# Moving eight bias-table matmuls to the start of a hybrid decoder block, and staging the second chunk's input in two rings

## The chip, the cores and the metric

The kernel runs on one core of one Trainium2 chip. The metric is the device time of one execution in microseconds, as the median of several runs. The profile is one further execution, taken by the hardware profiler; its span runs from the first to the last instruction. The engines are called as the profile calls them: PE (TensorE, matmuls; PEld are its weight loads), DVE (VectorE), ACT (ScalarE), POOL (GpSimd) and SP (SyncE, which here only issues DMAs). ACT issues some DMAs too, on a queue of its own.

## What is computed

One layer of a decoder block on 2048 positions of width 1024, in float32. The input is normalised and projected once; three mixers (a state-space mixer, a convolution module and a sliding-window attention) read parts of that projection; their outputs go through one output projection and a gate.

```python
hn = rms_norm(x, pre_norm_w)
u = jnp.einsum('bld,de->ble', hn, w_in)
z, xbc, dt_raw, conf_in, conf_gate, q, k, v, attn_gate = split_columns(u)
y_ssd = ssd_mixer(z, xbc, dt_raw, ...)
y_conf = conformer_conv(conf_in, ...) * jax.nn.silu(conf_gate)
y_attn = sliding_window_attention(q, k, v, sinks, rel_bias) * jax.nn.silu(attn_gate)
h = x + rms_norm(concat(y_ssd, y_conf, y_attn) @ w_out, post_norm_w)
return h + (p @ w_ple) * jax.nn.sigmoid(h @ w_gate)
```

The change touches the attention's relative bias: each of the eight heads adds to its scores a bias that depends only on the distance between query and key, through 32 buckets:

```python
dist = q_idx + ATTN_BLOCK - s_idx
bias = rel_bias.astype(jnp.float32)[t5_bucket(dist)]
s = jnp.where(valid, s + bias, -jnp.inf)
```

## The kernel before

**Tiling.** The 2048 positions are four chunks of 512 (`TC`). Activations lie transposed, features on the 128 partitions, so that a projection of 128 output features for one chunk is a sum over eight blocks of 128 input features (`KD`). To reach float32 accuracy with matmuls in the faster fp32r type, each operand is split into a high part and a remainder (`ah`, `al` for activations, `whi`, `wlo` for weights); `proj` issues three matmuls for each block (L443, L444, L445): low by high, high by low, high by high. For `dt` two suffice (L469, L470).

**Order.** The input projection runs in two halves of two chunks each. In a half, `head_front` projects k, v, dt, B0 and C0 for the first chunk, then for the second, and then a fixed list of units (C0, A0, S0, S1, C1, ...) each loads its weights and runs over both chunks; C is the convolution, A attention, S the state-space heads. Work that follows a projection waits in `pending` as generators, which `advance` steps once for each few matmuls. The code gives a program order; a scheduler then writes each engine's instruction list from it, by program order among what it expects to be ready. Each engine runs its list strictly in order.

**The start.** The first chunk's input is loaded in four pairs of blocks (`x_pair`, into the ring `t4`: tag "t4", four buffers of 128x1024). To begin early, `add_weighed` (ACT L392, DVE L393) multiplies it by the norm's weight only; the norm's per-position factor follows later: `sumsq_x` squares and adds (ACT L400, DVE L402), `rstd_cols` sums over partitions by matmul (L159), `make_row` transposes, stores the row to DRAM and `load_row` reads it back on all partitions (L186); it is applied when the projections leave PSUM (`evict`, DVE L478). For the second chunk, `pre_stats(1)` computes the row from another copy of the input (`xn`, also in `t4`; ACT L411), and `pre_apply(1)` loads the row into `acc`, the input pairs into the ring `gl` (two buffers), multiplies (DVE L433), and splits into `ah` and `al` (ACT L190, DVE L191).

**The bias tables.** `bias_tables` makes, for each head, one 128x384 table: a matmul of the head's 32 bucket values (and a row of -1e30 for distances out of the window), copied over 128 columns (`rbb`, DVE L547), with a one-hot matrix `oh` of 33x384. It is a float32 matmul with 33 rows, which TensorE runs in two passes (L549). ACT copies it from PSUM (L551) and SP stores it to `bias_d` in DRAM (L552), from where `attn_bias` reads it in a skewed pattern. The generator is put on `pending` after the first half's `head_front`, and uses PSUM tiles of the tag "m".

**PSUM and rings.** PSUM's eight banks are five of the tag "pp" (projections), two "m" and one "y". Other rings named below: "t" (`t512`, ten buffers of 128x512), `gl` (two) and `acc` (one).

Of the kernel before, what the change touches and what calls it, by code (L numbers as in the profile page):

```python
# [8 lines left out]
F32 = mybir.dt.float32  # L9
# [5 lines left out]
P = 128  # L15
# [3 lines left out]
TC = 512  # L19
# [3 lines left out]
NEG = -1e30  # L23
# [38 lines left out]
def hybrid_block_kernel(  # L62
# [15 lines left out]
    nc = tc.nc  # L78
    V, A, G, PE = nc.vector, nc.scalar, nc.gpsimd, nc.tensor
# [8 lines left out]
    def ps(tag):  # L88
        return psum.tile([P, TC], F32, tag=tag, name=f"ps_{tag}", bufs=PSB[tag])
# [4 lines left out]
    def t512(name, dtype=F32):  # L94
        return wk.tile([P, TC], dtype, tag="t", name=name, bufs=10)

    def t1024(name):
        return wk.tile([P, 2 * TC], F32, tag="t4", name=name, bufs=4)

    def pair(t):  # L100
        return t.rearrange("p (k t) -> p k t", k=2)

    def act_tiles():

        return act.tile([P, 2, TC], F32R, tag="ah", name="ah"), act.tile([P, 2, TC], F32R, tag="al", name="al")
# [5 lines left out]
    bias_d = dram.tile([8, P, 384], F32, name="bias_d")  # L111
# [10 lines left out]
    def pc(name, i=0, n=1):  # L122
        o, w = _par[name]
        return par_sb[:, o + i:o + i + n]
# [57 lines left out]
    def load_row(row, rb_=None):  # L182

        if rb_ is None:
            rb_ = t512("rb_")
        nc.sync.dma_start(out=rb_, in_=row.partition_broadcast(P))  # L186
        return rb_

    def split(hi, lo, src):
        A.copy(hi, src)  # L190
        V.tensor_tensor(out=lo, in0=src, in1=hi.bitcast(F32), op=ALU.subtract)  # L191
# [21 lines left out]
    pending = []  # L213
# [132 lines left out]
    with ExitStack() as c1:  # L346
        per = c1.enter_context(tc.tile_pool(name="per", bufs=1))
# [13 lines left out]
        def flush(n):  # L361
            while n > 0 and conv_q:
                if next(conv_q[0], "end") == "end":
                    conv_q.pop(0)
                else:
                    n -= 1
# [7 lines left out]
        def x_pair(c, i, tile_=None):  # L374
            x_ = pair(t1024("x2") if tile_ is None else tile_[:, 0:2 * TC])
            nc.sync.dma_start(out=x_, in_=xT[2 * i:2 * i + 2, :, c * TC:(c + 1) * TC].rearrange("k p t -> p k t"))
            return x_

        def gl_tile():
            return tp.tile([P, 30 + 2 * TC], F32, tag="gl", name="gl", bufs=2)  # L380

        def acc_tile():
            return tp.tile([P, 2 * TC], F32, tag="acc", name="acc", bufs=1)
# [35 lines left out]
        def add_pair(c, src):  # L419
            hi, lo = act_tiles()  # L420
            split(hi, lo, src)
            for kk in range(2):
                hn[c].append((hi[:, kk, :], lo[:, kk, :]))

        def pre_apply(c):

            flush(1000)
            rb_ = load_row(rows[c], acc_tile()[:, 0:TC])
            hn[c] = []
            for i in range(4):  # L430
                x_ = x_pair(c, i, gl_tile())
                for kk in range(2):
                    V.scalar_tensor_tensor(out=x_[:, kk, :], in0=x_[:, kk, :], scalar=pc("prew", 2 * i + kk), in1=rb_, op0=ALU.mult, op1=ALU.mult)  # L433
                add_pair(c, x_)


        def proj(ws, c):
# [12 lines left out]
        def wtile(name):  # L450
            return load_w(w_in[TIDX[name]])

        def dt_tile():

            st = wp.tile([P, KD, P], F32, tag="wst", name="wst", bufs=2)
            nc.sync.dma_start(out=st, in_=w_in[TIDX["dt"]])
            hi = wp.tile([P, KD, P], F32R, tag="whi", name="whi", bufs=5)
            both = wp.tile([P, KD, P], F32R, tag="wlo", name="wlo", bufs=5)
            A.copy(hi, st)
            A.copy(both, st)  # L460
            V.tensor_tensor(out=both[:, :, 16:32], in0=st[:, :, 0:16], in1=hi[:, :, 0:16].bitcast(F32), op=ALU.subtract)
            return hi, both
# [45 lines left out]
        def group_tiles():  # L508
            return tuple(per.tile([P, 2 * TC], F32, tag=n, name=n, bufs=1) for n in ("Bn", "CT", "CBm"))
# [10 lines left out]
        def bc_back(p, bT, cT, Bn, CT, CBm):  # L520
# [13 lines left out]
                in1=tri.unsqueeze(1).to_broadcast([P, NB, P]),  # L534
                op=ALU.mult,
            )


        def bias_tables():
            oh = t512("oh")  # L540
            nc.sync.dma_start(out=oh[0:33, 0:384], in_=onehot)
            rb = per.tile([33, 8], F32, name="rb")
            V.memset(rb, NEG)
            nc.sync.dma_start(out=rb[0:32, :], in_=relb)
            for h in range(8):
                rbb = t512("rbb")[0:33, 0:P]
                V.tensor_copy(rbb, rb[:, h:h + 1].to_broadcast([33, P]))  # L547
                pb = ps("m")
                PE.matmul(pb[:, 0:384], lhsT=rbb, rhs=oh[0:33, 0:384], start=True, stop=True)  # L549
                gr = t512("gr")  # L550
                A.copy(gr[:, 0:384], pb[:, 0:384])  # L551
                nc.sync.dma_start(out=bias_d[h], in_=gr[:, 0:384])  # L552
                if h % 2:
                    yield


        def dt_back(half, p, dT, dtr, tabs):
# [389 lines left out]
        for half in range(2):  # L947
            chunks = [2 * half, 2 * half + 1]
            gB = {}
            if half == 0:  # L950
                w0 = {"k": wtile("k")}
                xs = [x_pair(0, 0)]
                w0["v"] = wtile("v")
                xs += [x_pair(0, i) for i in range(1, 4)]
                w0["dt"] = dt_tile()
                w0["B0"] = wtile("B0")
                hn[0] = []
                for i in range(4):
                    add_weighed(0, xs[i], i)
                ssum = sumsq_x(xs)  # L960
                rs_ = []
            else:
                w0 = {n: dt_tile() if n == "dt" else wtile(n) for n in ("k", "v", "dt", "B0")}
                rs_ = None
            dtr = tp.tile([P, 2 * NB, 16], F32, tag="dtr", name="dtr", bufs=1)
            tabs = tuple(tp.tile([P, 2 * NB, 16], F32, tag=n, name=n, bufs=1) for n in ("dt", "acs", "eat", "dec"))
            gB[0] = group_tiles()
            front = head_front(half, 0, chunks[0], w0, gB[0], dtr, tabs, rs_)
            if half == 0:
                next(front)  # L970
                (rows[0],) = make_row(rstd_cols(ssum, 1.0 / D, EPS))
                rs_.append(load_row(rows[0]))
                for _ in pre_stats(1):
                    pass
                pre_apply(1)
            else:
                next(front)
                pre_apply(chunks[1])
            drive(front, 2)
            if half == 0:  # L980
                pre_apply(0)
            drive(head_front(half, 1, chunks[1], w0, gB[0], dtr, tabs), 2)
            if half == 0:
                pending.append(bias_tables())

            for unit in ("C0", "A0", "S0", "S1", "C1", "A1", "S2", "S3", "G1", "C2", "A2", "S4", "S5", "C3", "A3", "S6", "S7"):
                kind, j = unit[0], int(unit[1])
                if kind == "A":
                    wts = (attn_bias(j), wtile(f"q{j}"), wtile(f"ag{j}"))
                    front = attn_front  # L990
                elif kind == "C":
                    gl = gl_tile()
                    wts = (wtile(f"a{j}"), wtile(f"b{j}"), wtile(f"cg{j}"), gl)
                    front = conf_front
                elif kind == "S":
                    wts = (wtile(f"x{j}"), wtile(f"z{j}"), gB[j // 4], tabs)
                    front = ssd_front
                else:
                    gB[1] = group_tiles()
                    wts = (wtile("B1"), wtile("C1"), gB[1])  # L1000
                    front = bc_front
                for p, c in enumerate(chunks):
                    drive(front(j, p, c, *wts), TAPS[kind])
                    if half == 0 and unit == "S7" and p == 0:
                        pre_apply(2)
                    if half == 1 and unit == "S7" and p == 0:
                        tail = prep(0, YS[0])
                        pending.append(tail)
                    if half == 1 and unit == "C2" and p == 0:
                        pending.append(stats(0))  # L1010
                if half == 0 and unit == "A3":
                    keep_tail(1)
                if half == 0 and unit in ("A2", "C3"):
                    pending.append(pre_stats(j))
# [10 lines left out]
    with ExitStack() as c2:  # L1025
# [4 lines left out]
        for c in range(NCHUNK):  # L1030
# [7 lines left out]
            for n, (dp, kg) in enumerate(steps):  # L1038
# [4 lines left out]
                for kk in range(4):  # L1043
                    yh, yl = ys[4 * kg + kk]
                    first, last = kg + kk == 0, kg == 3 and kk == 3
                    for dd in range(2):
                        i = 2 * kk + dd
# [157 lines left out]
```

## Time and profile before

| | |
|---|---|
| median of 3 runs | 1844.33 us (1840.27 to 1845.91) |
| profiled execution | 1850.51 us |
| its span | 1848.7 us |
| mean granted TensorE clock | 0.994 |
| busy: PE, DVE, ACT | 98%, 75%, 44% of the span |
| L549, the tables' passes | 16, first at 100.3 us |
| L543 to L552, loads of `rb` and `oh` issued | 23.7 and 97.8 us |

A row of grouped instructions reads: line, engine, operation, output from inputs, shapes, count, then busy time, mean nanoseconds of one, and the idle time before it with what ended it. A row of the timeline reads: start and length in us, engine, line, operation; "x2" merges two in a row. A row of the chain that ended last reads: start, length, what. The letter q behind an engine means its instruction queue, which issues DMAs and waits on semaphores.

### The profile page before, as it was taken

Reading aid. Unit: us, or ns where it says so; the run is one execution under the profiler, and the core shown is the slowest. Engines: PE = TensorE matmul, PEld = TensorE weight load, DVE = VectorE, ACT = ScalarE, POOL = GpSimd, SP = SyncE. Lnnn points to the kernel's source line nnn. Section 1 sums busy time; section 2 is a strip of 40 time slices with the busy share of each in tenths; the row PEclk is TensorE's granted clock in tenths of the full one; section 3 lists DMA queues with packets and bytes.
Section 4 is the critical chain, followed back from the end, with each engine's and each line's share of the span. In section 5 each row is a group of like instructions: output and inputs, shape, how many; then the busy total and the mean of one; then the engine's idle time right before and its main releaser. Section 6 shows DMA issues by size and latency. Waiting matters only on the chain.

```text
span 1848.7 us, 25168 instructions
## 1 busy us (share of the span) xinstructions
PE 1810.7 (98%) x9386; PEld 1461.6 (79%) x9386; DVE 1385.1 (75%) x2400; ACT 818.6 (44%) x1565; POOL 0.2 (0%) x4
## 2 busy tenths in 40 slices
PE   6999999999999999999999999999999999999998
PEld 5877787787888778878788887877888788887887
DVE  6859769759869875976975996988777867466543
ACT  5525425524726542542653371465444444343331
POOL 0000000000000000000000000000000000000000
PEclk9999999999999999999999999999999999999999
DMA  7443233224433433333332332346677766578554
GB/s 234 132 133 98 80 102 96 61 78 106 171 112 111 121 102 104 91 87 89 100 115 76 101 99 87 82 145 230 214 242 236 245 228 199 202 240 280 189 188 131
DMA packets 118982, 265.09 MB, mean 143 GB/s; under 512 B 12619, under 2 KB 20428, under 8 KB 118860
## 3 DMA queue, kind: packets, MB, share of 16 engines
q1 hardware_dynamic: 108428, 246.65, 40.9%
q10 hardware_dynamic: 10432, 16.83, 4.1%
q8 instruction: 74, 1.21, 0.3%
q14 instruction: 48, 0.39, 0.1%
HBM read 205.05 MB, written 39.50 MB: 132 GB/s over the span
## 4 chain that ended last, share of the span: by engine, by line
PE 78%; DMA 8%; DVE 6%; ACT 4%; issue 2%; ACTq 1%; SPq 0%; DVEq 0%
PE ps_pp L443 15%; PE ps_pp L444 14%; PE ps_pp L445 14%; PE ps_pp L1048 4%; PE ps_pp L1049 4%; PE ps_pp L1050 4%; PE ps_pp L208 3%; PE ps_pp L209 3%; PE ps_pp L207 3%; PE ps_m L766 2%; PE ps_y L940 2%; PE ps_y L838 2%; DMA Ab<-acs_d 2%; PE ps_y L937 2%; PE ps_m L816 1%
## 5 line engine op out<-in xcount | busy, mean ns | idle before, releaser
L443 PE MATMUL ps_pp<-al,whi 128*128 128x512 f32 x1344 | 536.6, 400 | 13.6 <-DVE al L393 10.4
L444 PE MATMUL ps_pp<-ah,wlo 128*128 128x512 f32 x1344 | 534.5, 398 | 0.0
L445 PE MATMUL ps_pp<-ah,whi 128*128 128x512 f32 x1344 | 534.1, 397 | 0.0
L191 DVE TENSOR_TENSOR wlo<-wst,whi 128x1024 fp32r<-128x1024 f32 x214 | 234.1, 1102 | 179.8 <-ACT whi L190 179.4
L443 PEld LDWEIGHTS ps_pp<-al,whi 128*128 128x128 f32 x1344 | 254.4, 189 | 73.1 <-DVE al L393 10.4
L190 ACT CAST whi<-wst 128x1024 fp32r<-128x1024 f32 x214 | 202.9, 951 | 242.0 <-DMA wst<-in_w_gate_dram 86.1
L691 DVE SCALAR_TENSOR_TENSOR acc<-gl,par_sb,acc 128x1024 f32<-128x1024 f32 x240 | 307.3, 1280 | 2.3
L444 PEld LDWEIGHTS ps_pp<-ah,wlo 128*128 128x128 f32 x1344 | 254.6, 189 | 55.8 <-issue 6.5
L445 PEld LDWEIGHTS ps_pp<-ah,whi 128*128 128x128 f32 x1344 | 254.5, 189 | 54.4 <-issue 4.9
L489 DVE SCALAR_TENSOR_TENSOR cv<-raw,par_sb,cv 128x512 f32<-128x512 f32 x144 | 107.6, 747 | 22.7 <-ACT cv L487 22.0
L208 PE MATMUL ps_pp<-ah,wlo 128*128 128x512 f32 x256 | 100.2, 391 | 3.7 <-DVE wlo L191 3.7
L1048 PE MATMUL ps_pp<-bl,whi 128*128 128x512 f32 x256 | 101.5, 399 | 0.6 <-ACT whi L190 0.6
L1048 PE MATMUL ps_pp<-al,whi 128*128 128x512 f32 x256 | 100.4, 393 | 0.7 <-DVE al L191 0.7
L1049 PE MATMUL ps_pp<-bh,wlo 128*128 128x512 f32 x256 | 101.1, 395 | 0.0
L1050 PE MATMUL ps_pp<-bh,whi 128*128 128x512 f32 x256 | 100.7, 394 | 0.0
L207 PE MATMUL ps_pp<-al,whi 128*128 128x512 f32 x256 | 100.1, 391 | 0.6 <-ACT whi L190 0.5
L1049 PE MATMUL ps_pp<-ah,wlo 128*128 128x512 f32 x256 | 100.1, 391 | 0.0
L1050 PE MATMUL ps_pp<-ah,whi 128*128 128x512 f32 x256 | 100.0, 390 | 0.0
L209 PE MATMUL ps_pp<-ah,whi 128*128 128x512 f32 x256 | 99.7, 389 | 0.0
L796 ACT ACTIVATE S<-S,nm 128x256 f32<-128x256 f32 (+1 forms) x128 | 62.8, 492 | 80.0 <-DVE nm L782 74.6
L903 ACT ACTIVATE Ab<-Ab,acs 128x128 f32<-128x128 f32 x256 | 82.4, 391 | 0.4
L937 PE MATMUL ps_y<-Ab,xd 128*64 128x128 f32 x512 | 61.5, 282 | 2.0 <-issue 2.0
(235 smaller groups left out, 2592.1 us busy)
## 6 DMA issues: line engine op xcount, KB each, us to landing
wst<-in_w_in_dram SPq DMA_DIRECT2D x88, 512.0 KB, 3.5
wst<-in_w_out_dram SPq DMA_DIRECT2D x64, 512.0 KB, 5.1
Ab<-acs_d SPq DMA_DIRECT2D x64, 256.0 KB, 4.5
ysd<-y_d SPq DMA_DIRECT2D x32, 512.0 KB, 5.5
wst<-in_w_gate_dram SPq DMA_DIRECT2D x32, 512.0 KB, 3.5
gl<-in_xT_dram SPq DMA_DIRECT2D x16, 512.0 KB, 4.0
qh<-qh ACTq DMA_DIRECT2D x64, 128.0 KB, 2.4
ql<-ql ACTq DMA_DIRECT2D x64, 128.0 KB, 2.4
```

The costliest lines, as they stand in the source:

```text
L190: A.copy(hi, src)
L191: V.tensor_tensor(out=lo, in0=src, in1=hi.bitcast(F32), op=ALU.subtract)
L207: PE.matmul(out, lhsT=hi[:, k, :], rhs=al, start=start and k == 0, stop=False)
L208: PE.matmul(out, lhsT=lo[:, k, :], rhs=ah, start=False, stop=False)
L209: PE.matmul(out, lhsT=hi[:, k, :], rhs=ah, start=False, stop=stop and k == nk - 1)
L443: PE.matmul(o_, lhsT=hi[:, k, :], rhs=al, start=k == 0, stop=False)
L444: PE.matmul(o_, lhsT=lo[:, k, :], rhs=ah, start=False, stop=False)
L445: PE.matmul(o_, lhsT=hi[:, k, :], rhs=ah, start=False, stop=k == KD - 1)
L691: V.scalar_tensor_tensor(out=acc, in0=gl[:, k:k + 2 * TC], scalar=pc("ccw", j * 31 + k), in1=acc, op0=ALU.mult, op1=ALU.add)
L1048: PE.matmul(pj[dd], lhsT=hi[:, i, :], rhs=yl, start=first, stop=False)
L1049: PE.matmul(pj[dd], lhsT=lo[:, i, :], rhs=yh, start=False, stop=False)
L1050: PE.matmul(pj[dd], lhsT=hi[:, i, :], rhs=yh, start=False, stop=last)
```

## The change

The tables are computed at the start. `bias_tables` now runs up to its `yield` before `proj` is even defined, ahead of the first projection in program order: its two small loads go to ACT's DMA queue; `rbb` for all eight heads is one copy into a `gl` buffer; the eight matmuls write to eight different PSUM tiles, five "pp", two "m" and the one "y"; odd ones are evicted by DVE, even ones by ACT; four results lie in `t` buffers, two in `acc` and two in the other `gl` buffer. The stores to `bias_d` are placed after `pre_stats(1)`.

Since the `gl` ring is used by that, `pre_apply(1)` gets its four input pairs ready-made: the first two in `gl`, the other two in `t4`, all four issued ahead of the row load. The other calls of `pre_apply` stay as they were.

```diff
-        def pre_apply(c):
+        def pre_apply(c, xs=None):
 
             flush(1000)
             rb_ = load_row(rows[c], acc_tile()[:, 0:TC])
             hn[c] = []
             for i in range(4):
-                x_ = x_pair(c, i, gl_tile())
+                x_ = xs[i] if xs else x_pair(c, i, gl_tile())
...
+        def bias_tables():
+
+            rb = per.tile([33, 8], F32, name="rb")
+            nc.scalar.dma_start(out=rb[0:32, :], in_=relb)
+            oh = t512("oh")
+            nc.scalar.dma_start(out=oh[0:33, 0:384], in_=onehot)
+            V.memset(rb[32:33, :], NEG)
+            rbb = gl_tile()[0:33, 0:2 * TC].rearrange("p (h d) -> p h d", d=P)
+            V.tensor_copy(rbb, rb.unsqueeze(2).to_broadcast([33, 8, P]))
+            pairs = [acc_tile(), gl_tile()]
+            grs = [t512("gr")[:, 0:384] if h < 4 else pairs[h // 2 - 2][:, h % 2 * 384:(h % 2 + 1) * 384] for h in range(8)]
+            for h, gr in enumerate(grs):
+                pb = ps("pp" if h < 5 else "m" if h < 7 else "y")
+                PE.matmul(pb[:, 0:384], lhsT=rbb[:, h, :], rhs=oh[0:33, 0:384], start=True, stop=True)
+                if h % 2:
+                    V.tensor_copy(gr, pb[:, 0:384])
+                else:
+                    A.copy(gr, pb[:, 0:384])
+            yield
+            for h, gr in enumerate(grs):
+                nc.sync.dma_start(out=bias_d[h], in_=gr)
+
+        tables = bias_tables()
+        next(tables)
...
-        def bias_tables():
-            oh = t512("oh")
-            nc.sync.dma_start(out=oh[0:33, 0:384], in_=onehot)
-            rb = per.tile([33, 8], F32, name="rb")
-            V.memset(rb, NEG)
-            nc.sync.dma_start(out=rb[0:32, :], in_=relb)
-            for h in range(8):
-                rbb = t512("rbb")[0:33, 0:P]
-                V.tensor_copy(rbb, rb[:, h:h + 1].to_broadcast([33, P]))
-                pb = ps("m")
-                PE.matmul(pb[:, 0:384], lhsT=rbb, rhs=oh[0:33, 0:384], start=True, stop=True)
-                gr = t512("gr")
-                A.copy(gr[:, 0:384], pb[:, 0:384])
-                nc.sync.dma_start(out=bias_d[h], in_=gr[:, 0:384])
-                if h % 2:
-                    yield
...
-                pre_apply(1)
+                next(tables, None)
+                pre_apply(1, [x_pair(1, i, gl_tile() if i < 2 else None) for i in range(4)])
...
-            if half == 0:
-                pending.append(bias_tables())
```

## The prediction

> **What bounds the kernel now.** I read the page first (shares, then the chain that ended last), then TensorE's waits, the chain and the timeline of the first 120 us, and busy times by stretch.
>
> ```profile
> span 1848.7 us, 25168 instructions
> PE 1810.7 (98%) x9386; PEld 1461.6 (79%) x9386; DVE 1385.1 (75%) x2400; ACT 818.6 (44%) x1565; POOL 0.2 (0%) x4
> PE 78%; DMA 8%; DVE 6%; ACT 4%; issue 2%; ACTq 1%; SPq 0%; DVEq 0%
> ```
>
> TensorE is busy 98% of the span and carries 78% of the chain: a microsecond taken from its stream is a microsecond of the time, unless it comes out of one of its waits. Within the first 150 us the list of waits by engine and line (total, times, longest) shows two over 0.4 us:
>
> ```profile
> PE ps_pp L443 <- DVE al L393: 10.4, 1, 10.4
> PE ps_pp L443 <- DVE al L191: 3.2, 1, 3.2
> ```
>
> The first is the load of the first inputs and weights; into it the change moves work. The second is the wait for the second chunk's activations. How TensorE runs around both, and at the bias tables (columns: stretch, then busy us and count for PE, PEld, DVE, ACT, POOL, then granted clock, DMA share, GB/s):
>
> ```profile
> 10.44:17.05 6.61, 6.57 (x15) 4.53 (x16) 5.96 (x9) 6.61 (x12) 0.00 (x0) 1.00 0.94 344
> 17.05:24.70 7.65, 7.65 (x35) 6.35 (x34) 5.85 (x9) 7.22 (x12) 0.00 (x0) 1.00 0.73 244
> 41.60:45.07 3.47, 0.28 (x3) 0.00 (x1) 3.47 (x6) 2.21 (x3) 0.00 (x0) 0.90 0.26 60
> 45.07:51.10 6.03, 6.03 (x16) 4.86 (x17) 5.17 (x9) 1.07 (x2) 0.00 (x0) 0.50 0.54 173
> 112.60:116.10 3.50, 3.50 (x9) 2.83 (x9) 0.69 (x1) 1.47 (x3) 0.00 (x0) 0.51 0.67 221
> ```
>
> Full-speed 512-column matmuls come every 0.23 us (chain rows below). From 10.44 to 17.05 only 14 start (the count of 15 takes in the one at the border): half speed and two stalls, though the clock column, which knows nothing before the first recorded change, says 1.00. After the second wait 6.0 us run at a granted 0.50, and from 112.6 on 3.5 us at 0.51.
>
> **The change part by part.**
>
> *The tables leave their old place.* The chain there (start, us, what):
>
> ```profile
> 100.40 0.84 PE ps_m L549 x2
> 101.24 0.43 PE ps_pp L443
> 101.67 0.24 PE ps_pp L444
> ...
> 111.84 0.84 PE ps_m L549 x2
> 112.68 0.72 PE ps_pp L443
> 113.41 0.43 PE ps_pp L444
> ...
> 115.97 0.31 PE ps_pp L444
> 116.28 0.23 PE ps_pp L445
> ```
>
> From 100.40 to 116.28, 15.88 us, the chain holds the eight tables (two passes each) and 26 projection matmuls. At 0.23 us these 26 need 6.0, so the tables cost 15.88 - 6.0 = 9.9 us: 8 x 0.84 = 6.7 themselves, 0.20 more for the matmul behind each (0.43 for 0.23), and the half-speed stretch 112.6 to 116.1, which follows 12 us more than half filled by tables. VectorE and ScalarE have nothing that would take the bound over there: nobody waits for them in the waits above. I take the whole 9.9; the least is the 6.7 of the passes.
>
> *The tables at their new place.* What they wait for, from the start of the program:
>
> ```profile
> 1.17 0.42 SPq L120 DMA_DIRECT2D par_sb<-in_par_dram  x1
> 3.40 0.22 ACT L136 ACTIVATE par_sb<-par_sb 128x16 f32<-128x16 f32 x1 [1.09 <-DMA par_sb<-in_par_dram]
> 3.64 0.17 DVE L134 TENSOR_SCALAR par_sb<-par_sb 128x8 f32<-128x8 f32 x1
> 6.88 1.22 DVE L191 TENSOR_TENSOR wlo<-wst,whi 128x1024 fp32r<-128x1024 f32 x1 [3.08 <-ACT whi L190]
> 8.88 1.33 ACT L392 ACTIVATE ah<-x,par_sb 128x512 fp32r<-128x512 f32 x2 [2.03 <-DMA x<-in_xT_dram]
> 46.71 0.85 PE ps_m L505 x4
> 56.83 0.44 PE ps_m L505 x4
> 91.25 0.94 PE ps_m L530 x8
> ```
>
> Two small loads on ScalarE's queue, about 0.4 us each to issue, ahead of everything else there: with the 2.2 us that the parameters took (1.17 to 3.40) they are in by 3.5. VectorE is free from 3.8; the widened copy rbb, 1024 columns in one instruction instead of eight of 128, takes some 1.1 us (the 1024-column split takes 1.22) and fits in before the split at 6.88. So TensorE starts on the tables at about 5.0, a time at which it has nothing to do.
>
> How long they take there no row shows, since the tables ran at full speed. Low end: 0.84 each. Back to back I estimate a full-speed 384-column pass from L530 (eight 128-column passes in 0.94): 3 x 0.1175 = 0.35, a table 0.71. At half speed four transposes take 0.85 against 0.44, a factor 1.93: 1.36 a table. High end: 0.84 x 1.93 = 1.62. TensorE starts the program at half speed (first projection), so I take 1.36: 10.9 us, from 5.0 to 15.9. The first projection follows in TensorE's queue and slips from 10.44 to 15.9, by 5.5.
>
> Does the clock rise meanwhile? In the row it fell, at 112.6, after 12 us of tables with full matmuls between: a table (33 of 128 rows) seems to count for little. So I let the first projection pay its own ramp. Three ramps stand above, 6.6, 6.0 and 3.5 us, mean 5.4. Without the old stalls that is 12.6 matmuls at 0.43, which need 2.9 at full speed: 2.5 lost. Before, 14 matmuls (3.2 at full speed) took 6.6: 3.4 lost. That gives 0.9 back.
>
> The Trainium skill (TensorE: Matmul & The Clock Gate, Part 1: The HAM clock gate) says that sustained matmul activity of about one 3.4 us window releases the clock, whatever the number of matmuls. Read literally, the tables themselves warm the clock, and the sum would be that of the first rival below. The trace agrees on a fall after little activity, but no run here shows tables alone.
>
> *Evictions on all eight banks.* No table waits for a copy, so the eight follow each other. But the four ScalarE copies and four VectorE copies stand in first-in first-out queues ahead of casts and splits of the first projection:
>
> ```profile
> L551 ACT COPY gr<-ps_m 128x384 f32<-128x384 f32 x8 | 3.8, 480 | 8.0 <-PE ps_m L549 8.0
> ```
>
> 0.48 each. ScalarE is idle until 8.88 but full from there to 17.05 (6.61 of 6.61). If the seventh table's copy (matmul ready at 14.5) is queued ahead of the first activations' cast, that cast runs at 15 instead of 8.88, its split ends at 16.6 and the value-weights' split at 19.4. Price: nothing if they interleave, up to 2 us if both queues block. I take 1.0. The old copies fall away at 101 to 113, where they hid.
>
> *Stores and the staged input.* The stores move from 101 to 113 us to SP's queue in the start; loads of pairs 2 and 3 of the second chunk move from behind the release of the gl ring (45 us) to the t4 ring, free once the squares of xn are taken.
>
> ```profile
> bias_d<-gr SPq DMA_DIRECT2D x8, 192.0 KB, 2.9
> gl<-in_xT_dram SPq DMA_DIRECT2D x16, 512.0 KB, 4.0
> SPq L186 <- DMA row<-rt: 7.6, 2, 7.3
> ```
>
> 1.5 MB and 1 MB more ahead of the row load, and eight issues on SP. SP stands still 7.3 us before the row load that precedes the second chunk's, and DMA is at 0.73 and 0.26 in the two later stretches: hidden, zero. Without that cover it is 2.5 MB at 344 GB/s, 7.4 us. Pairs 2 and 3 are wanted only after 45 us, and TensorE waits for nothing over 0.4 us from there to 150: the earlier loads bring nothing by themselves. The moved gr, rbb and oh hold five of ten t buffers, acc and both gl until their stores land near 20 us; their next users act after 30, except the squares' sq tiles, which keep five buffers for ScalarE running one or two ahead: zero.
>
> The second wait stays: its chain starts in TensorE's own queue.
>
> ```profile
> 25.58 0.79 PE ps_m L159 x8
> 29.28 0.64 ACT xn L411
> 33.55 1.15 DMA row<-rt
> 34.71 6.40 DMA acc<-row
> 41.14 2.74 DVE gl L433 x4
> 43.88 1.15 DVE al L191
> ```
>
> L159 stands behind the first projection and slips with it, and so do the work that TensorE does meanwhile and the wait.
>
> *Sum.* -9.9 + 5.5 - 0.9 + 1.0 = -4.3 us. The profiled execution took 1850.5 (span 1848.7), so 1846.2 for it; it is 6.2 above the median 1844.3, and on the median the sum gives 1840.0. The forecast's own range, from 4.5 to 6 us for the start and 1.28 to 1.62 a table, is 1837 to 1843.
>
> **The rivals.**
>
> First, the tables warm the clock. From 5.0, 5.4 us at half speed (four tables) and four at 0.71: done at 13.2. The first projection slips 2.8, loses no ramp (-3.4), pays 1.0 for the queues: +0.4. 9.9 - 0.4 = 9.5 gained, 1834.8. For it: the first stretch warmed with stalls in it. Against: the fall at 112.6. This is also what the rule quoted above would give.
>
> Second, the tables land late. The same table load of 1 KB, behind big loads on SP's queue at 23.71, took 8.0 us:
>
> ```profile
> 23.71 0.42 SPq L544 DMA_DIRECT2D rb<-in_relb_dram  x1
> DMA to landing us min/median/max: 8.0/8.0/8.0
> ```
>
> Issued at 1.2 and landed at 9.2, tables from 10.3 to 21.2: slip 10.8, net +1.0, 1845.3, and 1847.4 at 1.62 a table. It decides from a start after 9.3 us. Against: the small parameters landed in 2.2.
>
> Third, slower: the row for the second chunk queues behind stores and staged inputs. Place: 34.71 to 41.14. Its 6.40 us, against 4.0 for a gl load of 512 KB, twice its bytes, speak for a queue there already. At the full 7.4 us the net is +3.1, 1847.4; it decides once the row is 4.3 us later relative to TensorE.
>
> Fourth, that wait shrinks. TensorE being later, the big loads are further ahead, and the row could land in the 4.0 us of a gl load, 2.4 sooner. The 3.47 us of wait become 1, perhaps too short for the clock to fall, and half of the 6.03 us at half speed is gone too: 2.4 + 3.0 = 5.4 more, 1834.6. Against: the staged loads go the same way.
>
> Fifth, the change does not do what it says: TensorE's order is written by a scheduler, and if the eight land among the first projection's matmuls they cost there what they cost now: 1844.3.
>
> **How the numbers follow.** Forecast 0.48; clock warmed 0.16; late tables 0.10; row behind 0.11; wait shrunk 0.12; not moved 0.03. About 0.3%, 5.5 us, is what a measurement of this kernel tells from no change. Faster by more: the first and fourth rival and 0.10 of the forecast, 0.38. Slower by more: the upper tails of the second and third, 0.08. Within: 0.54. The range 1834 to 1847 reaches past the first and fourth rival and leaves out most of the third and the tails, under 0.2.
>
> **What would show it.** In the changed trace: eight table pairs alone from about 5 us, 1.3 to 1.6 us apart, the first projection at about 16, half speed for some 5 us behind it; no half-speed stretch in the C0 unit near 110; the second wait near 47 us, about 3 long. Wrong if pairs come 0.7 apart before 12 us, if the tables start after 9, or if the second wait is gone or above 7.

## The result and the profile after

The changed kernel takes 1850.49 us (median of 20 runs, 1845.47 to 1855.96) against 1844.37 for the kernel before on the same chip (20 runs, 1840.27 to 1850.46): a ratio of 1.0036, 95% interval 1.0026 to 1.0047. It is slower by 6 us, where 4 us faster were forecast, and lies outside the range given. The profiled execution of the changed kernel took 1849.43, a little under that of before (1850.51), which lay at the slow end of its own spread; so the medians carry the sign, and the two traces are read for places and mechanisms only.

The page of the changed kernel, first lines and the chain that ended last:

```profile
span 1847.6 us, 25144 instructions
PE 1808.9 (98%) x9386; PEld 1463.4 (79%) x9386; DVE 1386.4 (75%) x2397; ACT 816.9 (44%) x1561; POOL 0.2 (0%) x4
PE 78%; DMA 9%; DVE 7%; ACT 4%; issue 2%; ACTq 1%; SPq 0%; DVEq 0%
```

Nothing here tells the two kernels apart, except DMA's and DVE's shares of the chain, each a point higher. TensorE's waits in the first 150 us do (total, times, longest):

```profile
PE ps_pp L469 <- ACT whi L190: 6.0, 1, 6.0
PE ps_pp L450 <- DVE gl L445: 3.7, 1, 3.7
PE ps_m L531 <- DVE vT L504: 3.4, 1, 3.4
```

The old start wait of 10.4 us is 3.7 now, and the tables fill what it left. The second wait, 3.2 us for the activations (`al`), has become two: 3.4 us for `vT`, then 6.0 us for `whi`, which is the high part of a *weight* tile. The chain of the start (start, length, what):

```profile
0.73 2.12 DMA rb<-in_relb_dram
2.94 0.70 DVE gl L445
3.68 6.76 PE ps_pp L450 x10
10.45 2.56 PE ps_m L450 x4
13.01 1.28 PE ps_y L450 x2
14.29 0.72 PE ps_pp L469
```

Two passes, one table, take 1.28 us from the first to the last; the first projection follows without a gap. By stretch, with the columns of the prediction's table (the clock column again says 1.00 until the first recorded change, here at 19.0):

```profile
14.29:18.85 4.56, 4.56 (x11) 3.59 (x12) 4.53 (x7) 4.56 (x9) 0.00 (x0) 1.00 0.43 126
42.00:53.00 11.00, 4.49 (x15) 2.80 (x14) 9.79 (x14) 6.86 (x7) 0.00 (x0) 0.54 0.78 239
110.00:116.00 6.00, 6.00 (x28) 4.99 (x27) 1.87 (x2) 2.09 (x3) 0.00 (x0) 1.00 0.25 87
```

The ramp is 4.6 us (11 matmuls), the stretch near 110 us runs at full speed, and between 42 and 53 TensorE does 4.5 us of work in 11, at a granted 0.54. Most of what the first 100 us lose goes there. TensorE's own timeline at that place, and ScalarE's last cast before it resumes (start, length, what, and in brackets the idle time before it):

```profile
38.02 0.39 PE L471 MATMUL ps_pp<-ah,whi 128*128 128x512 f32 x1
41.83 0.63 PE L531 MATMUL ps_m<-cst_sb,vT 128*128 128x128 f32 x4 [3.43 <-DVE vT L504]
...
49.11 1.22 PE L469 MATMUL ps_pp<-al,whi 128*128 128x512 f32 x2 [5.98 <-ACT whi L190]
...
48.02 1.04 ACT L190 CAST whi<-wst 128x1024 fp32r<-128x1024 f32 x1
```

The cast at 48.02 waits for the weights of the projection C0 that `head_front` runs behind B0 (`w0["C0"]`; it is not the convolution unit C0 of the list of units). Where was their load? SP's queue in the changed kernel:

```profile
26.66 0.40 SPq L376 DMA_DIRECT2D gl<-in_xT_dram  x1
27.16 0.86 SPq L376 DMA_DIRECT2D x<-in_xT_dram  x1
34.26 0.34 SPq L186 DMA_DIRECT2D rb__266<-row  x1
34.70 0.38 SPq L376 DMA_DIRECT2D gl<-in_xT_dram  x1
35.12 0.46 SPq L376 DMA_DIRECT2D x<-in_xT_dram  x1
40.48 0.34 SPq L186 DMA_DIRECT2D acc<-row  x1
...
42.70 0.59 SPq L647 DMA_DIRECT2D K<-kl  x1
43.34 1.32 SPq L196 DMA_DIRECT2D wst<-in_w_in_dram  x2
```

and before:

```profile
22.77 0.89 SPq L196 DMA_DIRECT2D wst<-in_w_in_dram  x2
...
31.53 0.34 SPq L186 DMA_DIRECT2D rb__229<-row  x1
```

The first of the two loads at 43.34 is C0's. It stands behind the four staged pairs, two row loads and four K stores, of which the rows and stores wait for data that is not there yet. That is its place in program order, in both kernels: `head_front` asks for it after the K stores. Before, the scheduler, which writes SP's list too, had drawn it ahead of both rows, to 22.77, in front of SP's long stand; in the changed kernel it did not. Issued at 43.34, it takes 4.7 us to land, and 1.04 to cast. Without C0's weights TensorE has no filler for the time in which the first chunk's values wait for their row (the 3.4 us), and then none for the second chunk.

How far TensorE is at the k-th low-by-high matmul into a `ps_pp` tile (`ps_pp<-al,whi`; those of `dt` count too: L443 and L469 before, L469 and L495 after), start in us. From about the 32nd on the two kernels run their projections in different orders, so the rows there compare the amount of work done:

| k | 0 | 8 | 28 | 32 | 48 | 96 | 128 |
|---|---|---|---|---|---|---|---|
| before | 10.4 | 19.3 | 33.0 | 35.8 | 53.0 | 89.0 | 121.8 |
| after | 14.2 | 22.0 | 35.0 | 49.1 | 63.0 | 98.8 | 120.6 |
| difference | +3.8 | +2.7 | +2.0 | +13.3 | +9.9 | +9.8 | -1.2 |

In these two executions the start costs 2.7, the waits some 7 more net, and the place of the old tables returns 11.0; in that are the 3.5 us at half speed that the profiled execution of before had there.

### The profile page after: what moved, and what is told of

The parts are those of the page before. It is cut to its first block, busy times and chain, and to the rows that moved or that the text cites. A ratio compares the mean times of both kernels' runs of the same rounds, so it can differ in the third digit from the quotient of the medians.

```text
span 1847.6 us, 25144 instructions
## 1 busy us (share of the span) xinstructions
PE 1808.9 (98%) x9386; PEld 1463.4 (79%) x9386; DVE 1386.4 (75%) x2397; ACT 816.9 (44%) x1561; POOL 0.2 (0%) x4
## 4 chain that ended last, share of the span: by engine, by line
PE 78%; DMA 9%; DVE 7%; ACT 4%; issue 2%; ACTq 1%; SPq 0%; DVEq 0%
PE ps_pp L469 15%; PE ps_pp L470 15%; PE ps_pp L471 15%; PE ps_pp L1055 3%; PE ps_pp L1057 3%; PE ps_pp L1056 3%; PE ps_pp L208 3%; PE ps_pp L209 3%; PE ps_pp L207 3%; PE ps_m L774 2%; PE ps_y L948 2%; PE ps_y L945 2%; PE ps_y L846 2%; DMA wst<-in_w_out_dram 2%; DVE wlo L191 2%
## 5 line engine op out<-in xcount | busy, mean ns | idle before, releaser
L469 PE MATMUL ps_pp<-al,whi 128*128 128x512 f32 x1344 | 534.1, 398 | 6.0 <-ACT whi L190 6.0
L469 PEld LDWEIGHTS ps_pp<-al,whi 128*128 128x128 f32 x1344 | 253.5, 189 | 63.1 <-issue 8.3
```

The lines of the kernel that those rows point to most:

```text
L469: PE.matmul(o_, lhsT=hi[:, k, :], rhs=al, start=k == 0, stop=False)
```

## The experiments

All ratios are to the kernel before, timed on the same chip between the same runs, with 95% intervals. Theory 1: C0's load behind the rows and stores makes the loss. Its rivals: the later projection by itself, the staged input by itself, or the bytes moved into the start.

**The tables alone, and the staged input alone.**

```diff
# e1: the changed kernel with
-                pre_apply(1, [x_pair(1, i, gl_tile() if i < 2 else None) for i in range(4)])
+                pre_apply(1)
# e2: the kernel before with that line the other way round, and pre_apply(c, xs=None)
```

> The tables moved to the start, the second chunk's input loaded as before (two gl buffers in turn). Theory 1 (the weights of C0 stand in SP's queue behind the second chunk's row and the K stores, and the projection waits for them): here C0's load stands ahead of the first row load in SP's order, so the waits of 3.4 and 6.0 us near 38 to 49 us are not there, and what is left is 9.9 us saved at 100 us less about 3.8 us of slip at the start: 1838 to 1841, 10 us under the changed kernel. Theory 2 (the staged loads and the stores crowd the DMA queues): also faster than the changed kernel, but the stores still crowd, so 1842 to 1847. Theory 3 (the tables cost at the start what they cost before): 1844 or more.

> Only the staging: four input pairs of the second chunk in two gl and two t4 buffers, tables in their old place. Theory 1: C0's load keeps its place ahead of the row loads, so nothing changes, 1843 to 1846, with the wait before the second chunk's first matmul at about 3 us. Theory 2: a megabyte more ahead of the rows delays them and the time grows, 1847 to 1850.

e1: 1841.31, ratio 0.9988 (0.9971 to 1.0006), just above theory 1's range. e2: 1843.49, 1.0004 (0.9989 to 1.0020). Neither half is slower. Loads on SP in e1, with TensorE's longest wait behind the start, then SP in e2:

```profile
27.35 0.93 SPq L196 DMA_DIRECT2D wst<-in_w_in_dram  x1
...
34.22 0.33 SPq L186 DMA_DIRECT2D rb__266<-row  x1
...
40.65 0.33 SPq L186 DMA_DIRECT2D acc<-row  x1
...
PE ps_pp L470 <- DVE wlo L191: 1.6, 1, 1.6
```

```profile
23.96 0.89 SPq L196 DMA_DIRECT2D wst<-in_w_in_dram  x1
...
32.49 0.34 SPq L186 DMA_DIRECT2D rb__229<-row  x1
```

In both, C0's load is ahead of the first row. e1 has every table matmul, every store and the slip of the first projection, so these are not the loss. Nor is the late row of the second chunk by itself: in e1 it goes into `acc` at 40.65, as late as in the changed kernel (40.48), and behind the start TensorE waits 1.6 us at most. Only with the two parts together is the load not drawn ahead; why the scheduler decides so is not shown.

**C0's weights early in the changed kernel.**

```diff
-                w0["C0"] = wtile("C0")
+                if "C0" not in w0:
+                    w0["C0"] = wtile("C0")
...
+                w0["C0"] = wtile("C0")
                 next(tables, None)
                 pre_apply(1, [...])
```

> The changed kernel with one line more: C0's weights are loaded ahead of the stores in program order. Theory 1: the waits of 3.4 and 6.0 us become one of about 3 us, and with it goes part of the half-speed stretch behind: 1838 to 1841, 10 us under the changed kernel. Theory 2 or 3: unchanged, 1849 to 1851.

1839.85, ratio 0.9984 (0.9968 to 1.0000): against the changed kernel's 1.0036, 0.52% or 9.6 us (some 6 to 13 by the two intervals), from the place of one load. TensorE's waits, and two issues on SP:

```profile
PE ps_pp L469 <- DVE al L191: 3.6, 1, 3.6
...
PE ps_m L531 <- DVE vT L504: 1.8, 1, 1.8
```

```profile
21.58 0.33 SPq L196 DMA_DIRECT2D wst<-in_w_in_dram  x1
...
38.08 0.46 SPq L186 DMA_DIRECT2D acc<-row  x1
```

The wait for `whi` is gone. What stays is the wait for `al` as before, 0.4 longer, and 1.8 for `vT`: the row goes into `acc` at 38.08 (before: 34.71).

**The same load held back in the kernel before.** This is the mechanism without any other part of the change (the edit is shortened).

```diff
-            w0["C0"] = wtile("C0")
+            with tc.issue_after(held.ins):      # held: the last K store, first half only
+                w0["C0"] = wtile("C0")
```

> The kernel before with nothing changed but the order on SP's queue: C0's weight load is held behind the four K stores of the first chunk, as it stands in the changed kernel; tables and inputs are as before. If the place of that load makes the loss (theory 1), TensorE waits twice near 35 to 46 us, and the time grows by 6 to 9 us: 1850 to 1853. If the crowding by stores and staged inputs makes it (theory 2), this is at most 2 us slower, since neither is here.

1851.93, ratio 1.0052 (1.0034 to 1.0070), 9.6 us slower. SP's loads, and TensorE's waits, with its first matmul for C0:

```profile
33.71 0.33 SPq L186 DMA_DIRECT2D acc<-row  x1
...
38.13 1.07 SPq L196 DMA_DIRECT2D wst<-in_w_in_dram  x2
```

```profile
PE ps_m L505 <- ACT cv L487: 4.1, 1, 4.1
...
PE ps_m L505 <- DVE vT L478: 2.1, 1, 2.1
...
43.03 1.22 PE L443 MATMUL ps_pp<-al,whi 128*128 128x512 f32 x2 [0.17 <-ACT whi L190]
```

The wait of 4.1 us ends at a transpose of `dT` and is put down to `cv`; the projection C0 itself begins at 43.03, as soon as its `whi` is cast. The row goes into `acc` at 33.71, earlier than before (34.71), so a late row has no part in this. Undoing it in the one kernel and doing it in the other give the same size. Theory 1 stands: the place of the load makes the loss.

How it makes it is shown only in part. In the traces the changed kernel stands 4.4 us behind e3 at the 96th and at the 128th matmul of the table above (98.8 for 94.4, 120.6 for 116.2), about as much as its two waits are longer (9.4 us for 5.4); at the end its span is 9.1 longer (1847.6 for 1838.5). The rest seems to go with the clock. The mean granted clock over all runs is 0.9926 in the changed kernel and 0.9962 in e3, 0.9927 in e5 and 0.9962 in the kernel before beside it; 0.0036 of 1848 us is 6.6 us, an estimate from above, since the clock is also low while TensorE waits. Within e5, the four runs at a clock of 0.995 or 0.996 take 1844.84 to 1846.44 us, the eight at 0.988 to 0.993 take 1850.03 to 1857.36, and the kept trace is one of the four. No run holds the clock fixed, and why it should be lower over the whole execution when one load is late in the first 50 us stays open.

**What the tables cost in their old place.**

```diff
-                pb = ps("m")
-                PE.matmul(pb[:, 0:384], lhsT=rbb, rhs=oh[0:33, 0:384], start=True, stop=True)
-                A.copy(gr[:, 0:384], pb[:, 0:384])
+                V.memset(gr[:, 0:384], 0.0)
```

> The kernel before without the eight table matmuls and their evictions; the tables are filled with zeros by VectorE (the bias is left out). It prices the tables in their old place: 9.9 us by the chain, so 1834 to 1835. If the time is above 1838, the saving that the prediction counted on was too large and theory 3 gains.

1835.27, ratio 0.9958 (0.9944 to 0.9973): the tables cost 0.42%, 7.7 us where 9.9 were forecast; the interval, 5.0 to 10.3 us, does not exclude 9.9.

**One matmul in place of eight.** The bias has only 8 x 384 different values: one matmul with the table itself as `lhsT` gives them, and the copy over 128 rows can be made by the store. Run at the start (e6), and in the old place (e7).

```diff
+            PE.matmul(pb[0:8, 0:384], lhsT=rb, rhs=oh[0:33, 0:384], start=True, stop=True)
+            A.copy(gr[0:8, 0:384], pb[0:8, 0:384])
+            nc.scalar.dma_start(out=tab, in_=gr[0:8, 0:384])
+            yield
+            for h in range(8):
+                nc.sync.dma_start(out=bias_d[h], in_=tab[h].partition_broadcast(P))
```

> One matmul for all eight heads (8 columns of weights, result 8x384) at the start, copied to a small DRAM table that is stored to bias_d by eight broadcasting DMAs; input not staged. One table of 1.3 us from about 3.7 is over before 10.4, so nothing slips, and the 8 us that the tables cost in their old place are saved: 1834 to 1837. If the place, not the number of matmuls, were what counts, it would be no better than the kernel with C0 early, 1840.

> The same one matmul in the tables' old place, behind the first half's head_front. It costs about 1 us there and no half-speed stretch: 1835 to 1838, within 1 or 2 us of the one at the start. If a single interruption is enough to lower the clock, 1839 or more.

e6: 1840.99, 0.9993 (0.9977 to 1.0008), a miss; e7: 1838.27, 0.9977 (0.9960 to 0.9995), just above its range. In e6, with hardly anything of the tables left on TensorE, a wait has grown, and SP shows why:

```profile
PE ps_pp L463 <- DVE al L191: 5.3, 1, 5.3
```

```profile
33.69 0.34 SPq L186 DMA_DIRECT2D rb__240<-row  x1
34.08 3.50 SPq L451 DMA_DIRECT2D bias_d<-tab  x4
37.68 0.53 SPq L186 DMA_DIRECT2D acc<-row  x1
```

Four stores of the bias stand between the two row loads: 3.5 us of issue on the path to `al`, the same queue again.

**These stores held behind the K stores, without and with a warm TensorE.** e11 is e6 with `next(tables, None)` under `tc.issue_after(held.ins)`, `held` being the last K store of the second chunk; e12 adds six idle 128-row float32 matmuls at the start.

> The one-matmul start of e6 (the bias is made at the start by one small matmul), but its broadcast stores go to SP's queue only behind the second chunk's K stores. If early stores on SP made e6's long wait for the second chunk's activations (5.3 us), that wait is 3 us or less here and the time is 1835 to 1838, as where the small matmul stands in its old place (1838.3). If the wait came from something else, the time stays at e6's 1839 to 1842.

> The run before, with six full-height idle matmuls at the start that raise the clock before the first projection. The first projection should begin near 10.3 us at full speed and be 2 to 3 us ahead by its eighth output tile. If TensorE's own stream sets when the second chunk's activations are ready, the gain stays and the time is 1832 to 1835. If the chain of row loads sets it, the second wait grows by what the start saved, and the time is that of the run before within 2 us.

e11: 1833.40 on a chip where before takes 1841.87, ratio 0.9964 (0.9952 to 0.9976), so 1837.7 where before takes 1844.37; e12: 1837.62, 0.9972 (0.9958 to 0.9986). e11's wait and row load:

```profile
PE ps_pp L463 <- DVE al L191: 2.1, 1, 2.1
```

```profile
35.08 0.38 SPq L186 DMA_DIRECT2D acc<-row  x1
```

The wait falls from 5.3 to 2.1 with the row 2.6 us earlier, and e11 has the lowest ratio of the versions that compute the bias, though its interval overlaps those of e7, e9 and e12. e12 (its trace is of its slowest run) is 2.7 us ahead of the kernel before at its 20th block (24.8 against 27.5), and then waits 4.9 for `al`, which is ready at 44.8 (e11: 43.5): the chain of row loads, not TensorE, sets that moment, and the warm start gains nothing that can be measured.

**Tables at full height, and a warm start by itself.** e8 is e3 with `rb` and `oh` padded with zero rows to 128; e10 is e8 with the zero fills ahead of all else; e9 is e7 with the six idle matmuls.

> The kernel with C0 early, its eight tables taken with 128 rows instead of 33 (95 rows of zeros, same result). If the clock counts rows in use, it rises inside the tables after one or two windows: the later pairs 0.7 apart, the first projection at about 12 instead of 14.2 and at full speed, 1835 to 1838. If not, all eight pairs 1.3 apart as before and 1839 to 1841.

> The kernel with one table matmul in the old place, and ahead of the first projection six idle matmuls over all 128 rows (ones by zeros, float32, 512 columns, result unused) from about 2.3 us on. If rows in use are what the clock counts, it has risen by 6 to 9 us, the first projection starts near 10 us with 0.23 us a matmul from the first on, and the 2 to 3 us that its half-speed stretch costs are saved: 1834 to 1836.5, against 1838.3 without them. If zeros or float32 don't count, or the late first weights bind instead, 1837 to 1840.

> The changed kernel with C0 early and 128-row tables (zeros in 95 rows), with the two zero fills ahead of all other VectorE work, so that the small loads go out at 1 to 1.5 us and not at 2.8. If the loads land by 4 us, the tables start there, the clock rises at 7 to 11, the first projection starts near 11.5 at full speed instead of 14.2 at half: 4 to 6 us under the 33-row version's 1840, 1834 to 1836. If the loads are late again (behind the big ones), 1842 or more.

e8: 1845.27, 1.0018 (1.0000 to 1.0035); e9: 1839.59, 0.9974 (0.9960 to 0.9989); e10: 1843.44, 1.0003 (0.9988 to 1.0019). All three miss the time given for a clock that has risen, and yet the traces show that it rose. In e8 the zero fill delayed the load of `oh` to 2.83 us, behind the big ones (chain, then TensorE by stretch):

```profile
2.83 7.13 DMA oh<-in_onehot_dram
```

```profile
10.10:13.45 3.35, 3.35 (x6) 1.84 (x7) 1.30 (x3) 1.45 (x3) 0.00 (x0) 1.00 1.06 397
13.45:16.78 3.33, 3.33 (x13) 2.01 (x11) 3.28 (x6) 2.73 (x6) 0.00 (x0) 1.00 0.50 111
```

In the first 3.35 us of tables six passes run, in the next 3.33 thirteen (one of each count on the border): the clock rose inside the tables. In e9 likewise:

```profile
2.29:8.40 6.11, 6.11 (x7) 2.52 (x8) 1.47 (x5) 2.46 (x7) 0.00 (x0) 1.00 0.94 300
8.40:10.30 1.90, 1.90 (x7) 0.92 (x5) 1.56 (x3) 1.90 (x3) 0.00 (x0) 1.00 1.06 410
```

and its projection begins at 10.2 at full speed. e9 reads as e7 in the median all the same. In e10 the tables start at 4.03, the first projection at 11.5 at full speed, and TensorE is 1.5 us ahead of before at the 8th block; then it waits 4.3 us for `al`, and stands 2.3 us behind at the 40th.

## Why the prediction was wrong

**The step that failed** is "hidden, zero" under *Stores and the staged input*, together with "the second wait stays". I priced what SP has to issue (eight stores) and what the DMA engines have to move (2.5 MB), and neither e1 nor e2, which have one of the two each, is slower than before. (That both together are wholly hidden is not shown: in e3 the second chunk's row still goes out 3.4 us later than before.) I did not price the order: SP's list is written anew by the scheduler, and a load that TensorE needs, drawn ahead before, can be left behind work that waits. The missing term is C0's weights, issued 20.6 us later (43.34 for 22.77), 9.6 us of time by e3 and by e5, of which the traces show 4.4 as longer waits. The forecast sum with this term is -4.3 + 9.6 = +5.3; measured, +6.1. An outcome slower by more than 5.5 us had been given a chance of 0.08.

**The rest of the sum** is tested by e3, which has the whole change and not that term: 1839.85, on a chip where before takes 1843.46, so -0.16% (interval -0.32% to 0), 3 us (0 to 5.9), for -4.3 forecast. Term by term:

- *Old place*: 9.9 forecast, 7.7 by e4. For the profiled execution the reading was right: from the 96th to the 128th matmul it takes 32.8 us, e4's 22.8. But I took its half-speed stretch at 112.6 as the price of every execution. The lower bound of the prediction, 6.7, is nearer to 7.7; e4's interval holds both.
- *Start of the tables*: 3.68 instead of 5.0. The loads landed by 2.9 and `rbb` took 0.69, not 1.1.
- *One table*: 1.28 instead of 1.36. With the earlier start, which is the larger part, they end at 14.29 instead of 15.9, and the slip is 3.8 instead of 5.5.
- *The ramp*: 4.56 us for 5.4 forecast, and the slip shrinks to 2.7 by the 8th block: 1.1 back, for 0.9.
- *Queues*: 1.0 forecast, none seen; the first projection follows the last table at 14.29 at once.

So start and ramp cost 2.7 where 5.6 were forecast, and the two errors partly cancel, which is luck: -7.7 + 2.7 = -5.0. The 2 us that e3 lacks against this are inside its interval. They would fit its longer waits (5.4 in all against 3.2, the row into `acc` 3.4 us later), but that link was only argued for e3; it was shown for e6 by e11. One sum of the prediction is off, without bearing on this: a start at 4.5 and 1.28 a table give 1838.8, not 1837, as the low end.

**The rivals.** The third was the one on the right engine: it had the second chunk's row behind stores and staged inputs on SP. The row is later (40.48 for 34.71), and its split of `al` begins 3 us later (46.90 for 43.88), but e1 has the same late row without the loss: the load that decided was C0's weights, which the rival does not name; its bound, 7.4 us of bytes, was a bound for the wrong thing. The first, that the tables warm the clock, is refuted as written: after 10.6 us of tables without a stop the projection still ran 4.6 us at half speed. The Trainium skill (TensorE: Matmul & The Clock Gate, Part 1: The HAM clock gate) has sustained activity of about 3.4 us release the clock whatever the number of matmuls. With all 128 rows in use that fits e8 (3.3 us), less well e10 (some 5 us) and e9 (6.1 us); with 33 rows the trace disagrees. The second, late tables, did not occur in the change (0.73 to 2.85 for `rb`), but e8 shows that its margin was at most 1.6 us of issue time (`oh` issued at 2.83 for 1.2). The fourth and fifth did not occur.

**What was to show it.** Eight pairs alone, half speed of about 5 us behind them, and no half speed near 110 were there, the pairs 1.28 apart and the first projection at 14.3, earlier than the 16 expected. The second wait "about 3 long" was not: 9.4 us in two pieces, which is over the 7 named as a sign of error.

## What to carry to other kernels

When work is moved in program order and a scheduler writes the queues, compare the whole list of the in-order DMA queue before and after, not only its number of issues and bytes: ask of every weight load what now stands ahead of it, and for what that waits. In program order, a load with no input of its own belongs ahead of loads that wait for a row and of stores: then its place does not hang on what the scheduler expects. And before speeding up the front of a pipeline, look what ends the next wait: if it is a chain of row loads, the front's gain becomes wait.

## What was not expected of the hardware

- The clock seems to weigh a matmul by the rows in use. Float32 passes with 33 rows, 16 in a row over 10.6 us, stayed at 1.28 us a pair; zero-padded to 128 rows they doubled their rate after 3.3 us (e8) and some 5 us (e10), with nothing but zeros in 95 of the rows. The start does not explain it: e10's tables begin at 4.03, those with 33 rows at 3.68. Matmuls whose one operand is all zeros warmed it as well (e9).
- Whether the clock falls in a wait is not set by the wait's length alone. After 3.2 us of waiting the profiled execution of before ran 6.0 us at half speed, and e11 fell after 2.1; e4, with the same stream as before up to there and a 3.1 us wait, did not fall, and its lead over before grew from 0.6 us at the 40th block to 3.5 at the 44th. What seems to count is how the wait lies against a fixed grid: in each of the fourteen traces every recorded change of the clock lies a whole number of steps of 3.41 us from the first one, and a stretch at half speed lasts one, two or three steps. The wait of e4 straddles a border, with 1.3 us idle in one step and 1.8 in the next; before and e11 have 2.5 and 2.1 us idle within one step. The step of e11, then the two of e4 and the stretch behind them:

```profile
41.10:44.50 3.40, 1.35 (x7) 0.79 (x6) 3.40 (x5) 2.76 (x3) 0.00 (x0) 1.00 0.35 93
...
39.20:42.60 3.40, 2.09 (x11) 1.46 (x10) 2.10 (x4) 1.24 (x2) 0.00 (x0) 1.00 0.86 232
42.60:46.00 3.40, 1.57 (x9) 1.34 (x10) 3.40 (x4) 2.16 (x3) 0.00 (x0) 1.00 0.11 39
44.40:50.40 6.00, 5.97 (x28) 4.98 (x29) 5.37 (x9) 1.56 (x2) 0.00 (x0) 1.00 0.52 175
```

  With 1.8 us idle in a step e3 and e4 kept the clock and e10 lost it, so the border lies near there; no run varies the idle time by itself. Single executions of one kernel therefore differ by several us, and one profile's half-speed stretch is not a price.
- A small load of the same bytes took 2.6 us when issued at 1.33 (e10) and 7.1 when issued at 2.83 (e8). In e8 the big loads of SP's queue go out ahead of it, which may be the reason; no run varies that by itself.
